# One reference token per block for the scan's scores, with the level-wise scan kept behind a branch, and sample states in fp32

## The chip, the cores and the metric

The kernel runs on one core of one Trainium2 chip. Its time is the device time of one execution in microseconds (us), lower is better. TensorE (PE) multiplies, VectorE (DVE) and ScalarE (ACT) work element by element, GpSimd (POOL) fills constants and issues some transfers, SyncE (SP) issues the others.

## The reference

One decoder layer is applied to 256 prompt tokens and to 32 sample tokens (8 sequences of 4): a SwiGLU feed-forward part, a mixer of two recurrences, and a second feed-forward part. All is fp32. The mixer's heads compute

```python
def gated_linear_scan(q, k, v, log_a, s0):
    """S_t = diag(exp(log_a_t)) S_{t-1} + k_t^T v_t ; o_t = q_t S_t."""
...
        diff = cum[:, :, :, None, :] - cum[:, :, None, :, :]
        decay = jnp.where(causal, jnp.exp(jnp.where(causal, diff, 0.0)), 0.0)
        scores = jnp.sum(qi[:, :, :, None, :] * ki[:, :, None, :, :] * decay, axis=-1)
        o = (jnp.einsum('bhts,bhsv->bhtv', scores, vi)
             + jnp.einsum('bhtd,bhdv->bhtv', qi * jnp.exp(cum), s))
...
        s_new = (jnp.exp(last[:, :, 0, :])[..., None] * s
                 + jnp.einsum('bhsd,bhsv->bhdv', ki * jnp.exp(last - cum), vi))
```

`cum` is the running sum of the log decays. The score of token t on token s therefore holds exp(cum_t - cum_s) for each of 128 key channels. There are 4 GLA heads (key width 128, value width 256, log decay = log-sigmoid / 16) and 8 HGRN heads (128 and 128; the lower bound of the gate is zero at depth one, so the log decay is a plain log-sigmoid). Prompt sequences start from zero states, sample sequences from given ones; final states of both are outputs.

## The kernel before

**Products with weights.** Activations are kept transposed, 128 channels by 288 tokens (256 prompt, 32 sample). Each weight tile is loaded by SP (lines 61 and 63, three buffers `raw`), split into a high and a low part by ACT (`wh`, line 86) and DVE (`wl`, line 87), and used in three PE products per 128x128 tile (lines 464 to 466, in the type that PE takes in one pass). `block` runs these products, four output tiles wide, and calls a `tick` after every 128 input rows, that is after every 12 products.

**The scans.** There are six scans, two heads each: two for GLA, four for HGRN. Each is a Python generator, and a `tick` advances the first one by one `yield`, so a scan's small products stand between the large ones of the blocks `qk1`, `v1`, `hfq`, `hi` and `gate`. The framework's scheduler may still move an instruction within an engine's program. Per scan:

- Scores, level by level: `own` (line 804) for a token with itself, then for h = 1, 2, ... 128 `score` multiplies the keys of the left halves with the queries of the right halves (line 839, four products of 64 columns; line 832 for h = 128; lines 845 and 849 for the samples at h = 1 and 2), `put` copies the valid entries into the score tile `Dg` or `Ds` with a mask (line 864 and others), and `update` (lines 820 to 824) multiplies the decay of one more level into queries, keys and the decay products `F`. No exponent of a positive number is ever taken.
- Output: `out` (lines 933 to 937) multiplies scores with values.
- Sample states: a state tile of 128x512 fp32 is loaded, `halve` (lines 959 and 960) splits it into high and low parts on ACT and DVE, and `sample` multiplies both by the masked queries `qm` (line 978, 64 weight columns, 256 moving columns, four per state tile). Lines 970 and 973 form the new state's update, line 982 adds it on DVE, line 984 stores it from POOL's queue. `inter_a` and `inter_b` (line 996) bring the result back to the transposed layout.
- `final` (line 946) forms the prompt's final state, `norm_a` to `norm_c` the head norm.

**Setup and end.** `setup` fills constants on POOL after the first norm of the mixer. The program's last work is `finish`, whose stores SP issues (lines 650 and 654).

Of the kernel before, what the change touches and what calls it, by code (L numbers as in the profile page):

```python
# [16 lines left out]
P = 128  # L17
# [17 lines left out]
X_EARLY = 12  # L35

# [77 lines left out]

@with_exitstack
def trunk_kernel(ctx, tc, x_prompt, x_sample, state_gla, state_hgrn, norm_gains, f1_in, f1_out, f2_in, f2_out,
                 mix_in, gla_up, gla_b, gla_norm, hgrn_gamma, hgrn_norm, mix_out, masks,
                 y_prompt, y_sample, sgp, shp, sgs, shs):
    nc = tc.nc
    V, S, G, PE = nc.vector, nc.scalar, nc.gpsimd, nc.tensor  # L120

# [535 lines left out]
    def mixer(pn, border):  # L657
        with ExitStack() as mx:
# [5 lines left out]
            def scan_pool():  # L664
                border.pools.close()
                sp.append(mx.enter_context(tc.tile_pool(name="scan", bufs=2, side="right", reuse_waits="tile")))
                its.append(sp[0].tile([P, 256], F32, name="it", bufs=1))
                for i in range(2):
                    vs32.append(sp[0].tile([P, 512], F32, name=f"vs{i}", bufs=1))

                    qm.append(sp[0].tile([P, 9 * 64], F32R, name=f"qm{i}", bufs=1))
            ones = {dv: cst.tile([P, P], F32R, name=f"ones{dv}") for dv in (256, 128)}
            mk = cst.tile([P, 576], U8, name="mk")
# [8 lines left out]
            Dg = cst.tile([P, 2, 2, P], F32, name="Dg")  # L682
            Ds = cst.tile([P, 2, TS], F32, name="Ds")
            Dflat = Dg.rearrange("p i a c -> p (i a) c")

            def setup():
                mi32 = sp[0].tile([P, 576], mybir.dt.int32, name="mi32", tag="Q", bufs=1)
# [3 lines left out]
                G.dma_start(mi32, masks[:, 0:576])  # L691
# [15 lines left out]
                G.tensor_copy(mk, mi32)  # L707
                for a in range(2):
                    G.memset(qm[a].bitcast(F32), 0.0)
                V.tensor_tensor(sel, ident[:, 0:TS], ident[:, TS:2 * TS], op=ALU.add)  # L710
                G.tensor_copy(bmask, bm32)
# [53 lines left out]
            def log_sigmoid(out, z):  # L765

                e = tmp.tile([P, T], F32, name="ls", tag="ls")
                S.activation(e, z, AF.Abs)
                act(e, e, AF.Exp, scale=-1.0)
                act(e, e, AF.Ln, bias=1.0)  # L770
                V.scalar_tensor_tensor(out, z, 0.0, e, op0=ALU.min, op1=ALU.subtract)

            def scan(d, Vt, V32, Vs, gla, ytile0, s0, sp_out, ss_out):
# [246 lines left out]
                def norm_c(a):  # L1020
                    r0 = tmp.tile([P, T], F32, name="r0", tag="lsg")
                    r1 = tmp.tile([P, T], F32, name="r1", tag="ls")
                    act(r0, mss[a][:, 0:T], AF.Ln, bias=epst)
                    act(r0, r0, AF.Exp, scale=-0.5)

                    S.activation(r1, r0, AF.Square)
                    V.scalar_tensor_tensor(r1, mss[a][:, 0:T], EPS, r1, op0=ALU.add, op1=ALU.mult)
                    V.scalar_tensor_tensor(r1, r1, -3.0, r0, op0=ALU.add, op1=ALU.mult)
                    for j in range(nv):
                        yt = y[ytile0 + a * nv + j]  # L1030
                        V.scalar_tensor_tensor(yt, yt, hgain[:, j:j + 1] if gla else hgain[:, 2:3], r1,
                                               op0=ALU.mult, op1=ALU.mult)
# [8 lines left out]
                for a in range(2):  # L1041
                    for b0 in range(0, NB, nb):
                        if b0 + nb < NB:
                            apart(a, b0 + nb)
                            halve(a, b0 + nb)
                        if b0 == 0:
                            final(a)
                        sample(a, b0)
                        if a == 0 and b0 == nb:
                            tp = key_t(1)  # L1050
                        yield
                        if a == 0 and b0 == nb:
                            key_e(1, tp)
                    if a == 0:
                        apart(1, 0)
                        halve(1, 0)
                    inter_a(a)
                    yield
                    inter_b(a)
                    norm_a(a)  # L1060
                    later.append([lambda: None, lambda: None, lambda a=a: norm_b(a), lambda a=a: norm_c(a)])
                    yield
                    if a == 0:
                        out(1)
                        yield
# [47 lines left out]
            def gla_decay(d, g):  # L1113
                for f in range(2):
# [5 lines left out]
                    log_sigmoid(z, z)  # L1120
                    act(d["f"][:, f, :], z, AF.Exp, scale=1.0 / 16.0)

            def ev_hgrn(d, g):
                def ev(f, ps):
# [14 lines left out]
                    V.tensor_scalar(d["f"][:, f, :], ls, omlb[:, hd:hd + 1], lb[:, hd:hd + 1], op0=ALU.mult, op1=ALU.add)  # L1139
                return ev  # L1140

            for g in range(2):
# [14 lines left out]
                gens.append((g, scan(d, *vt, True, 4 * g, state_gla[0][:, 2 * g:2 * g + 2],  # L1157
                                     sgp[0, 0, 2 * g:2 * g + 2], sgs[0][:, 2 * g:2 * g + 2]), True))
            ds, vts = {}, {}
            for kind, g in HORDER:  # L1160
# [8 lines left out]
                for j in list(ds):  # L1169
                    if j // 2 in vts:  # L1170
                        c = slice((j % 2) * 256, (j % 2 + 1) * 256)
                        vt, v32, vs = vts[j // 2]
                        gens.append((2 + j, scan(ds.pop(j), vt[:, :, c], v32[:, c], vs[:, c], False, 8 + 2 * j,
# [34 lines left out]

            for n in range(4):
                block(f"gate{n}", KT, xrhs, ev_gate(n), tick=(tick, tick, tick_silu, tick_last)[n])  # L1210
            for t in range(12, KT):
                split_y(t)
            act_set(AF.Sqrt)
# [70 lines left out]
```

## Time and profile before

| | |
|---|---|
| median of 3 runs | 2307.12 us (2306.62 to 2309.29) |
| span of the profiled execution, first to last instruction | 2303.8 us |
| median less span | 3.3 us |
| granted TensorE clock, mean | 0.998 |
| PE busy | 2287.0 us, 99% |
| DVE busy | 1415.0 us, 61% |
| ACT busy | 1018.9 us, 44% |
| POOL busy | 50.8 us, 2% |
| HBM | 363.62 MB read, 11.80 MB written |

The span is what the profile shows; the run's time has also what lies around it. A PE row's duration is that of one product through the array, and products overlap, so the time that a product holds PE is read from the distance between two starts. One fp32 product of the program makes two records (x8 in the trace for x4 in the program), one with high-low parts makes one, a transpose makes one.

### The profile page before, as it was taken

How to read it: one execution, taken by the hardware profiler on the slowest of the kernel's cores; microseconds unless marked ns; L12 is line 12 of the kernel's file. 1: busy time of each engine (PE TensorE's matmuls, PEld its weight loads, DVE VectorE, ACT ScalarE, POOL GpSimd, SP SyncE). 2: the span in 40 equal slices, each digit the busy share in tenths (PEclk: the TensorE clock that was granted, in tenths of full speed). 3: DMA queues.
4: the chain of work that ended last, by engine and by line, in shares of the span. 5: the costliest groups of instructions: out<-in, count | busy, mean ns of one | idle time of the engine just before them, and what ended most of it. 6: DMA issues, size and time to landing. Idle time of an engine off the chain costs nothing.

```text
span 2303.8 us, 42125 instructions
## 1 busy us (share of the span) xinstructions
PE 2287.0 (99%) x17352; PEld 2274.0 (99%) x17352; DVE 1415.0 (61%) x2303; ACT 1018.9 (44%) x1567; POOL 50.8 (2%) x97
## 2 busy tenths in 40 slices
PE   9999999999999999999999999999999999999998
PEld 8999999999999999999999999999999999999998
DVE  7545545554556468788888754854555455545545
ACT  6443333333334445454556654544333333333345
POOL 0000000000000001000000000100000000000000
PEclk9999999999999999999999999999999999999999
DMA  7555555555555545456465555455555555555553
GB/s 216 165 165 165 165 166 166 167 166 168 166 165 184 165 152 164 142 163 181 144 173 155 161 185 160 136 164 168 165 165 166 167 163 164 165 165 165 165 165 115
DMA packets 217008, 378.16 MB, mean 164 GB/s; under 512 B 15362, under 2 KB 52400, under 8 KB 216816
## 3 DMA queue, kind: packets, MB, share of 16 engines
q1 hardware_dynamic: 211264, 365.48, 52.4%
q0 software_dynamic: 3376, 9.81, 1.3%
q8 instruction: 136, 2.23, 0.4%
q10 hardware_dynamic: 2176, 0.18, 0.1%
q14 instruction: 56, 0.46, 0.1%
HBM read 363.62 MB, written 11.80 MB: 163 GB/s over the span
## 4 chain that ended last, share of the span: by engine, by line
PE 88%; issue 7%; DVE 2%; DMA 1%; POOL 1%; ACT 1%; DVEq 0%; POOLq 0%; ACTq 0%; SPq 0%
PE gate L464 9%; PE gate L466 9%; PE gate L465 9%; PE out L465 8%; PE out L466 8%; PE out L464 8%; PE up L466 8%; PE up L464 8%; PE up L465 8%; PE mo L466 1%; PE mo L464 1%; PE mo L465 1%; PE hfq L464 1%; PE hfq L465 1%; PE hfq L466 1%
## 5 line engine op out<-in xcount | busy, mean ns | idle before, releaser
L87 DVE TENSOR_TENSOR wl<-raw,wh 128x1024 fp32r<-128x1024 f32 (+1 forms) x674 | 821.7, 1220 | 627.4 <-ACT wh L86 624.7
L86 ACT ACTIVATE wh<-raw 128x1024 fp32r<-128x1024 f32 (+1 forms) x674 | 711.3, 1056 | 1067.3 <-PE gate L465 318.4
L465 PE MATMUL gate<-xl,wh 128*128 128x288 f32 x1660 | 489.1, 295 | 0.1
L466 PE MATMUL gate<-xh,wl 128*128 128x288 f32 x1660 | 489.1, 295 | 0.0
L464 PE MATMUL gate<-xh,wh 128*128 128x288 f32 x1660 | 488.6, 296 | 0.0
L465 PE MATMUL out<-hl,wh 128*128 128x288 f32 x1408 | 415.8, 295 | 0.0
L464 PE MATMUL out<-hh,wh 128*128 128x288 f32 x1408 | 415.6, 295 | 0.0
L466 PE MATMUL up<-xh,wl 128*128 128x288 f32 x1408 | 415.0, 295 | 0.0
L466 PE MATMUL out<-hh,wl 128*128 128x288 f32 x1408 | 415.0, 295 | 0.0
L464 PE MATMUL up<-xh,wh 128*128 128x288 f32 x1408 | 414.6, 294 | 0.3 <-DVE g L523 0.3
L465 PE MATMUL up<-xl,wh 128*128 128x288 f32 x1408 | 414.8, 295 | 0.0
L465 PEld LDWEIGHTS gate<-xl,wh 128*128 128x128 f32 x1660 | 311.9, 188 | 1.0 <-DVE xl L243 0.9
L466 PEld LDWEIGHTS gate<-xh,wl 128*128 128x128 f32 x1660 | 311.7, 188 | 0.0
L464 PEld LDWEIGHTS gate<-xh,wh 128*128 128x128 f32 x1660 | 310.6, 188 | 0.7 <-ACT xh L242 0.2
L464 PEld LDWEIGHTS out<-hh,wh 128*128 128x128 f32 x1408 | 264.6, 188 | 0.2 <-DVE u L531 0.2
L466 PEld LDWEIGHTS out<-hh,wl 128*128 128x128 f32 x1408 | 264.7, 188 | 0.0
L464 PEld LDWEIGHTS up<-xh,wh 128*128 128x128 f32 x1408 | 264.1, 188 | 0.6 <-DVE g L523 0.5
L465 PEld LDWEIGHTS out<-hl,wh 128*128 128x128 f32 x1408 | 264.5, 188 | 0.0
L466 PEld LDWEIGHTS up<-xh,wl 128*128 128x128 f32 x1408 | 264.2, 188 | 0.1
L465 PEld LDWEIGHTS up<-xl,wh 128*128 128x128 f32 x1408 | 264.1, 188 | 0.1
L583 DVE TENSOR_TENSOR y<-out,y 128x288 f32<-128x288 f32 x288 | 121.5, 452 | 104.5 <-PE out L466 101.7
L464 PE MATMUL hfq<-xh,wh 128*128 128x288 f32 x256 | 78.4, 306 | 0.0
(341 smaller groups left out, 2560.1 us busy)
## 6 DMA issues: line engine op xcount, KB each, us to landing
raw<-in_ffn_w_in_dram SPq DMA_DIRECT2D x352, 512.0 KB, 3.6
raw<-in_ffn_w_out_dram SPq DMA_DIRECT2D x176, 512.0 KB, 3.7
raw<-in_mix_w_in_dram SPq DMA_DIRECT2D x64, 512.0 KB, 3.7
raw<-in_mix_w_in_dram SPq DMA_DIRECT2D x96, 256.0 KB, 3.3
raw<-in_mix_w_out_dram SPq DMA_DIRECT2D x32, 512.0 KB, 3.7
out_dram<-s POOLq DMA_DIRECT2D x32, 256.0 KB, 3.1
s<-in_state_gla_dram SPq DMA_DIRECT2D x16, 256.0 KB, 4.0
s<-in_state_hgrn_dram SPq DMA_DIRECT2D x16, 256.0 KB, 3.3
```

Source lines behind the costliest of these rows:

```text
L86: i1 = self.nc.scalar.activation(h[:, c], raw[:, c], AF.Copy).ins
L87: i2 = self.nc.vector.tensor_tensor(l[:, c], raw[:, c], h[:, c].bitcast(F32), op=ALU.subtract).ins
L464: yield lambda: PE.matmul(dst, w[0][:, c:c + P], parts[0], start=start, stop=False)
L465: yield lambda: PE.matmul(dst, w[0][:, c:c + P], parts[1], start=False, stop=False)
L466: yield lambda: PE.matmul(dst, w[1][:, c:c + P], parts[0], start=False, stop=stop)
L583: V.tensor_tensor(y[k], ps, y[k], op=ALU.add)
```

## The change

`trunk_kernel` becomes a wrapper. It allocates `span` and `over`, runs the whole layer once (`trunk`, with `block_scan`), loads `over` into a register of every engine and, under `tc.If`, runs the whole layer again with the old scans. The second copy is in the program as a block that is jumped over when `over` is 0.

`block_scan` takes the place of `scan` in the first run. A running sum of the log decay is made by two instructions on DVE (`tensor_tensor_scan`), reset at each block of tokens: 256 for GLA, 64 for HGRN, 4 for a sample sequence. The sum at the block's middle token is subtracted, the queries are multiplied by exp(sum), the keys by exp(-sum), and the scores of a block are one product and one masked copy. For HGRN, factors between neighbouring blocks of 64 (`g6`, `g7`, `gk`, `gs`) give the other scores. The largest distance from the middle token is collected in `span` and compared with 60 at the end of the mixer; beyond that `over` is 1. Sums are clamped to ±60. The gates hand over the log decay rather than the decay.

The sample states stay in fp32: `run` multiplies all eight states of a head, one after the other, with 32 weight columns each, into four different groups of 32 output partitions in turn, and four products add the samples' own scores. State buffers `s0` go from 5 to 8, and loads are issued in the scan's first steps. `mi32` and its mask load go; `block_masks` makes the masks on POOL.

```diff
+def trunk_kernel(tc, *args):
+    with tc.tile_pool(name="guard", bufs=1) as pool:
+        span = pool.tile([P, 2, 12], F32, name="span")
+        over = pool.tile([1, 1], mybir.dt.int32, name="over")
+        trunk(tc, *args, (span, over))
+        again = tc.nc.values_load(over[0:1, 0:1], min_val=0, max_val=1)
+        with tc.If(again > 0, preferred_fallthrough_block=False):
+            trunk(tc, *args, None)
...
+            def block_scan(d, Vt, V32, Vs, gla, ytile0, s0, sp_out, ss_out):
...
+                for a in range(2):
+                    V.tensor_tensor_scan(f[:, a, :], resets[0 if gla else 1], f[:, a, :], 0.0, op0=ALU.mult, op1=ALU.add)
+                load_state()
+                yield
+                for x_, c in zip(blocks(f), (0, n)):
+                    h = x_.shape[3] // 2
+                    V.tensor_copy(col(mid, c, x_.shape[2]), x_[:, :, :, h - 1:h])
+                    V.tensor_tensor(x_, x_, col(mid, c, x_.shape[2]).broadcast_to(x_.shape), op=ALU.subtract)
+                for x_, c in zip(blocks(f), (0, 4)):
+                    s_ = col(span, c, x_.shape[2])
+                    for i, u in ((0, unit), (x_.shape[3] - 1, -unit)):
+                        V.scalar_tensor_tensor(s_, x_[:, :, :, i:i + 1], u, s_, op0=ALU.mult, op1=ALU.max)
+                V.tensor_scalar(f, f, SPAN / unit, -SPAN / unit, op0=ALU.min, op1=ALU.max)
+                act(ep, f, AF.Exp, scale=unit)
+                act(A, mid, AF.Exp, scale=unit)
...
+                act(f, f, AF.Exp, scale=-unit)
...
+                V.tensor_tensor(k, k, f, op=ALU.mult)
...
+                if gla:
+                    for a in range(2):
+                        ps = auxtile("sc")
+                        PE.matmul(ps[:, 0:TP], k[:, a, 0:P], q[:, a, 0:TP], start=True, stop=True, skip_group_check=True)
+                        PE.matmul(ps[:, TP:3 * P], k[:, a, P:TP], q[:, a, P:TP], start=False, stop=True,
+                                  skip_group_check=True)
+                        own(ps, a)
+                        V.copy_predicated(Dg[:, a], tri, ps[:, 0:3 * P])
+                        own_put(ps, a, a + 1)
+                        yield
+                else:
+                    for i in range(2):
+                        ps = auxtile("sc")
+                        for a in range(2):
+                            PE.matmul(ps[:, a * 192:(a + 1) * 192], k[:, a, i * P:(i + 1) * P], Qv[:, a, i, :],
+                                      start=a == 0, stop=True, skip_group_check=True)
...
+                    ps = auxtile("sc7")
+                    for a in range(2):
+                        PE.matmul(ps[:, a * P:(a + 1) * P], Kd[:, a, 0:P], q7[:, a, :], start=a == 0, stop=True,
+                                  skip_group_check=True)
...
+                def run(a):
+                    ss = auxtile("os")
+                    w = dv // 4
+                    for b in range(NB):
+                        r = slice(b % 4 * TS, (b % 4 + 1) * TS)
+                        PE.matmul(ss[r, 0:dv], qm[0][:, a, b * TS:(b + 1) * TS], states[a, b // nb * nb][:, b % nb, :],
+                                  start=b < 4, stop=False, skip_group_check=True)
+                    for i in range(4):
+                        PE.matmul(ss[i * TS:(i + 1) * TS, i * w:(i + 1) * w], Ds[:, a, :],
+                                  V32[:, a * dv + i * w:a * dv + (i + 1) * w], start=False, stop=True, skip_group_check=True)
+                    it = sp[0].tile([P, dv], F32, name="it", tag="it", bufs=1)
+                    S.activation(it, ss[:, 0:dv], AF.Copy)
+                    its_[a] = it
+
+                def out(a):
+                    po = auxtile("o")
+                    for j in range(nv):
+                        v = [Vt[:, t, a * dv + j * P:a * dv + (j + 1) * P] for t in range(2)]
+                        PE.matmul(po[:, j * TP:(j + 1) * TP], v[0], Dg[:, a, 0:TP], start=j == 0, stop=False,
+                                  skip_group_check=True)
+                        PE.matmul(po[:, j * TP + P:(j + 1) * TP], v[1], Dg[:, a, TP:3 * P], start=False, stop=True,
+                                  skip_group_check=True)
```

Three places show how the instructions move. The first is PE's program at the first HGRN scan's scores, before (`Q` and `k_h` are the queries and keys with the decay so far, 127x64 is the size of the result; the rows of the blocks between are left out):

```order
L804 MATMUL sc_d<-q_h_10939,k_h_10940 128x128 x4
...
L839 MATMUL sc_11921<-Q,k_h_10940 127x64 x4
L845 MATMUL sc_11921<-Q,k_h_10940 32x16 x2
L849 MATMUL sc_11921<-q_h_10939,k_h_10940 32x32 x2
...
L839 MATMUL sc_11964<-Q,k_h_10940 126x64 x4
L845 MATMUL sc_11964<-Q,k_h_10940 32x16 x2
...
L839 MATMUL sc_11999<-Q,k_h_10940 124x64 x4
```

The same place on PE now (`Qv` holds the queries with the factor to the block's middle, `Kd` the keys carried to the half's end):

```order
L1249 MATMUL sc<-Qv,k_h_10833 128x192 x2
L1228 MATMUL sc<-rp,k_h_10833 32x32 x2
...
L1249 MATMUL sc<-Qv,k_h_10833 128x192 x2
...
L1264 MATMUL sc_11854<-q_h_10832,Kd 128x128 x2
```

Nine stops of PE between the blocks' products become three, and 40 products become 8.

The second place is PE at the sample states of the first HGRN scan, before (`hl` is a split state, `qm` the masked queries, `sn` the new state's update):

```order
L973 MATMUL sn<-bd,ks 128x512
L978 MATMUL os<-hl,qm_9574 64x256 x4
L464 MATMUL hfq_0_11877<-xh_137,wh_12066 128x288
...
L973 MATMUL sn<-bd,ks 128x512
L978 MATMUL os<-hl,qm_9574 64x256 x4
```

And now, for the second head of that scan (`s` is a state as loaded, `Ds` the samples' own scores):

```order
L1347 MATMUL sn<-bd,ks 128x512
L1301 MATMUL os<-s_11952,qm 32x128 x4
L1301 MATMUL os<-s_12004,qm 32x128 x4
L1304 MATMUL os<-vs_9581,Ds 32x32 x4
L479 MATMUL hi_0_12123<-xh_130,wh_11899 128x288
```

The state products no longer stand with each state's update; eight of them and four more follow each other without a large product between.

The third place is DVE at the start of the first HGRN scan, now (`small` holds the block factors, `s` states and `sn` updates of the GLA scan before it):

```order
L1187 TENSOR_TENSOR Qv<-q_h_10832,ep 128x4x128
L1188 TENSOR_TENSOR rp<-q_h_10832,ep 128x64
L1193 TENSOR_TENSOR k_h_10833<-k_h_10833,f_h_10834 128x576
...
L1213 TENSOR_TENSOR Kd<-k_h_10833,small 128x512
L1215 TENSOR_TENSOR q_h_10832<-Qv,small 128x2x128
...
L1350 SCALAR_TENSOR_TENSOR s_11212<-s_11212,small,sn 128x256 x2
L1291 TENSOR_TENSOR bd<-ks,bmask 96x256
```

The scan's whole preparation stands on DVE ahead of the last four state updates of the GLA scan before it, while PE's score products of this scan stand behind that scan's last products.

On SP one register load of `over` stands between two loads of `mix_w_out` weights; on the other engines it stands at the end of the program, ahead of the branch.

More of the change, by code (lines that the diff above doesn't have):

```diff
@@ L35 @@
 X_EARLY = 12
+SPAN = 60.0
 class Weights:
@@ L706, in setup @@
                 G.memset(Ds, 0.0)
-                G.tensor_copy(mk, mi32)
-                for a in range(2):
-                    G.memset(qm[a].bitcast(F32), 0.0)
+                if not blockwise:
+                    G.tensor_copy(mk, mi32)
+                for t in qm:
+                    G.memset(t.bitcast(F32) if t.dtype == F32R else t, 0.0)
                 V.tensor_tensor(sel, ident[:, 0:TS], ident[:, TS:2 * TS], op=ALU.add)
+                if blockwise:
+                    for i in (2, 3):
+                        V.tensor_tensor(sel, sel, ident[:, i * TS:(i + 1) * TS], op=ALU.add)
                 G.tensor_copy(bmask, bm32)
@@ L1020, in norm_c @@
                 def norm_c(a):
[L1021 to L1032, printed above, removed]
+                    head_norm(mss[a], [y[ytile0 + a * nv + j] for j in range(nv)], gla)
                 tp = key_t(0)
```

284 lines of the change are left out of this document (269 added, 15 removed).

## The prediction

> **What bounds the kernel now.** The page of the profile comes first: its head, its first part (busy time by engine) and its fourth (the chain of work that ended last, by engine).
>
> ```profile
> span 2303.8 us, 42125 instructions
> PE 2287.0 (99%) x17352; PEld 2274.0 (99%) x17352; DVE 1415.0 (61%) x2303; ACT 1018.9 (44%) x1567; POOL 50.8 (2%) x97
> PE 88%; issue 7%; DVE 2%; DMA 1%; POOL 1%; ACT 1%; DVEq 0%; POOLq 0%; ACTq 0%; SPq 0%
> ```
>
> PE is busy all the time and carries the chain. The change lies in the mixer, so the second view is the windows: the mixer as a whole, a stretch full of scans, and one behind the last scan. The columns are the length, then busy time and instruction count of PE, PEld, DVE, ACT and POOL.
>
> ```profile
> 860.00:1440.00 580.00, 578.17 (x4477) 568.96 (x4476) 450.80 (x949) 311.61 (x635) 37.41 (x62) 1.00 0.54 162
> 1240.00:1300.00 60.00, 60.00 (x474) 58.83 (x474) 51.39 (x120) 34.44 (x75) 4.11 (x6) 1.00 0.48 140
> 1300.00:1360.00 60.00, 60.00 (x454) 60.00 (x454) 40.16 (x62) 36.70 (x56) 0.00 (x0) 1.00 0.59 185
> ```
>
> In the mixer PE misses 1.8 of 580 us, at a granted clock of 1.00. DVE comes next with 51.39 of 60 us where scans run and 40.16 where none does. A product taken from PE there is time taken from the kernel, as long as nothing else becomes later than PE; work taken from DVE, ACT or a DMA is not.
>
> **How I price a product.** The timeline of PE gives start and duration; what counts is the distance between starts. In steady state products of 288 columns stand 0.13 us apart. This is a stretch with `own` of one scan and the large products behind it:
>
> ```profile
> 1239.14 1.05 PE L804 MATMUL sc_d<-q_h,k_h 128*128 128x128 f32 x8
> 1239.95 0.38 PE L464 MATMUL gate<-xh,wh 128*128 128x288 f32 x1
> 1240.17 0.29 PE L465 MATMUL gate<-xl,wh 128*128 128x288 f32 x1
> 1240.29 0.29 PE L466 MATMUL gate<-xh,wl 128*128 128x288 f32 x1
> ```
>
> Four fp32 products (eight records) start at 1239.14, the next large one at 1239.95, and that one holds PE 0.22 us and not 0.13. So the stop costs 0.81 + 0.09 = 0.90 us, 0.225 a product of 128 columns. I use the same sum, distance plus 0.09, for each stop.
>
> **Scores.** Level h = 1, h = 4, h = 64 and h = 128 of a scan, each with the row that follows it:
>
> ```profile
> 1241.62 0.99 PE L839 MATMUL sc<-Q,k_h 128*127 128x64 f32 x8
> 1242.54 0.30 PE L845 MATMUL sc<-Q,k_h 128*32 128x16 f32 x4
> 1242.69 0.29 PE L849 MATMUL sc<-q_h,k_h 128*32 128x32 f32 x4
> 1242.91 0.40 PE L464 MATMUL gate<-xh,wh 128*128 128x288 f32 x1
> 1251.99 0.98 PE L839 MATMUL sc<-Q,k_h 128*124 128x64 f32 x8
> 1252.78 0.38 PE L466 MATMUL gate<-xh,wl 128*128 128x288 f32 x1
> 1266.31 0.68 PE L839 MATMUL sc<-Q,k_h 128*64 128x64 f32 x8
> 1266.92 0.40 PE L465 MATMUL gate<-xl,wh 128*128 128x288 f32 x1
> 1267.95 0.67 PE L832 MATMUL sc<-Q,k_h 128*128 128x128 f32 x4
> 1268.37 0.38 PE L466 MATMUL gate<-xh,wl 128*128 128x288 f32 x1
> ```
>
> That makes 1.38 for h = 1, 0.88 for h = 4, 0.70 for h = 64, 0.51 for h = 128. For h = 2 I take 1.2 (h = 1 without line 849), for the three levels between h = 4 and h = 64 their mean, 0.79 each. With `own`: 0.90 + 1.38 + 1.2 + 0.88 + 2.37 + 0.70 + 0.51 = 7.9 us a scan, 47.6 us for six.
>
> What replaces them needs a price for 256 columns. The prompt's final state of a GLA scan has it (two products, four records):
>
> ```profile
> 954.47 1.11 PE L946 MATMUL st<-Vg,kd 128*128 128x256 f32 x4
> 955.24 0.57 PE L970 MATMUL sn<-Vsg,bd 96*128 96x256 f32 x2
> ```
>
> 0.77 + 0.09 is 0.43 a product; 192 columns lie midway to 0.225, at 0.33. The samples' own scores have 32 weight columns: line 849 takes 0.22 + 0.09 = 0.31 for two, and the four products before line 845 take 0.92 where those at h = 4 take 0.79, so entering the 32-column form costs about 0.1. A GLA head then costs 0.43 + 0.225 + 0.26 = 0.92, an HGRN scan 4 x 0.33 + 0.41 + 2 x 0.225 = 2.2. Four heads and four scans: 12.3 us. The scores give back 47.6 - 12.3 = 35.3 us.
>
> **Outputs.** Lines 933 to 937 and the state products after them:
>
> ```profile
> 1211.80 0.38 PE L933 MATMUL o<-Dg,Vh 128*128 128x128 f32 x2
> 1212.24 0.39 PE L935 MATMUL o<-Dg,Vh 128*128 128x128 f32 x2
> 1212.46 0.31 PE L937 MATMUL os<-Ds,vs 128*128 128x32 f32 x2
> 1212.60 0.66 PE L978 MATMUL os<-hl,qm 128*64 128x256 f32 x4
> 1213.10 0.29 PE L464 MATMUL gate<-xh,wh 128*128 128x288 f32 x1
> ```
>
> 0.80 us for a head and half of 128 values, 16 of them. Now it is one product of 256 and one of 128 columns, 0.655: 2.3 us back. (Line 937's part is counted in `run`.)
>
> **Sample states.** From the same rows, the four products of line 978 take 0.50 us; at a GLA scan, in the first two rows here, 0.48. The third row groups all of them:
>
> ```profile
> 970.26 0.64 PE L978 MATMUL os<-hl,qm 128*64 128x256 f32 x4
> 970.74 0.29 PE L464 MATMUL v<-xh,wh 128*128 128x288 f32 x1
> L978 PE MATMUL os<-hl,qm 128*64 128x256 f32 x128 | 20.7, 282 | 0.0
> ```
>
> 32 stops of four, 15.4 us, go. `run` brings, for each of four GLA heads, eight fp32 products of 256 columns and four of 64; for each of eight HGRN heads eight of 128 and four of 32. If each waits for the one before it, that is 8 x 0.43 + 4 x 0.11 = 3.9 us a GLA head and 8 x 0.215 + 4 x 0.07 = 2.0 an HGRN head (0.11 between the 32-column price and that of 128 columns), 32 us in all, and 12 stops with two changes of form and a late large product, 0.3 each, 3.6 us. So 36 us in turn, and fp32 states are then 20 us worse than split ones.
>
> But consecutive products of `run` use four different strips of 32 output columns, and nothing in this trace does. Line 978 uses the first 64 columns alone, lines 845 and 849 the first 32, one after the other. The bounds are thus one product at a time (36 us) and four at a time (8 + 3.6 = 11.7 us). Between them I use the records: each fp32 product is two passes, both on the same strip and in program order, so the second pass of one can lie beside the first pass of the next, but not beside its own first. That hides half: 16 + 3.6 = 19.8 us. I take it as an estimate.
>
> The Trainium skill, "TensorEngine Tiling (Array Packing)", section Key Properties, says that tiles work independently and load and multiply in parallel, and that a change of tiling mode drains the engine. On the first, `run` would cost 11.7 us rather than 19.8; no run here shows it so far. On the second the trace agrees (the 0.1 us into the 32-column form).
>
> PE's sum: 35.3 + 2.3 + 15.4 - 19.8 = 33.2 us less.
>
> **What is hidden, and what is not.** The split of states (lines 959 and 960, 24.0 and 25.2 us on ACT and DVE), masked copies and level updates go; running sums, exponentials and factors come. They lie beside PE in both kernels. DVE loses, per scan, nine steps of two multiplications and a masked copy, and gains some nine wide operations:
>
> ```profile
> L959 ACT ACTIVATE hl<-s 128x256 fp32r<-128x256 f32 x64 | 24.0, 408 | 15.2 <-PE os L978 10.6 <-DMA s<-in_state_hgrn_dram 3.4 <-DMA s<-in_state_gla_dram 0.9
> L960 DVE TENSOR_TENSOR hl<-s,hl 128x256 fp32r<-128x256 f32 x64 | 25.2, 417 | 0.2
> L820 DVE TENSOR_TENSOR Q<-Q,F 128x256 f32<-128x256 f32 (+1 forms) x36 | 15.4, 427 | 15.5 <-PE sc L839 13.0 <-PE sc L845 2.4
> L882 DVE TENSOR_TENSOR Q<-q_h,f_h 128x576 f32<-128x576 f32 x4 | 3.0, 752 | 0.0
> L149 ACT ACTIVATE ls<-ls 128x288 f32<-128x288 f32 x56 | 22.5, 433 | 0.4
> ```
>
> No row shows a running sum; the nearest, 128x288 elementwise, takes 0.45 us, and up to double that changes nothing while PE bounds. What can cost is the chain from the running sum to the first score product: sums, subtraction, clamp, exponential on ACT twice, two multiplications, the block factors. At 0.45 to 0.9 for each sum, 0.75 for each wide step and 0.9 for each wide exponential (two of 0.433), with a dozen small ones of 0.2, it is about 9 us long. The generator gives it five or six steps of 12 products, 8 to 9.5 us; but in the program DVE does it ahead of the last four state updates of the scan before. I book 2 us for waits on it, between -2 (the waits that PE had in the mixer, 1.8 us) and 10.
>
> SP now waits for `over` with weight loads behind it. The longest wait of SP for a split is in this row, and PE does not wait behind it:
>
> ```profile
> SPq L63 <- DVE wl L87: 1258.7, 443, 13.7
> ```
>
> `over` stands some nine DVE instructions behind the split that frees the next buffer, about 6 us; three raw and four split tiles of 3.2 us lie ahead of PE. I book nothing, and 6 us as the bound without that cover.
>
> At the end every engine branches over the second copy of the layer, SP last. Its last rows:
>
> ```profile
> 2297.73 1.41 DVE L642 SCALAR_TENSOR_TENSOR zT<-zT,rc,xT 128x512 f32<-128x512 f32 x2
> 2299.68 0.89 SPq L654 DMA_DIRECT2D out_dram<-zT  x2
> ```
>
> SP issues until 2300.57 and the span ends at 2303.8, while the stores land. The other engines' register load and branch fit into that; SP's far jump comes after the landing. No row has such a jump: its bounds are nothing and the 3.2 us that a transfer and the end take here; I take 2. The Trainium skill, "Runtime: NRT & Kernel Launch", section Instruction fetch mechanics, says that a taken branch out of the prefetched window forces a fetch of the target before execution goes on; that would lie within these bounds, and no run here shows it yet.
>
> **The sum.** 33.2 - 2 - 2 = 29.2 us less: a span of 2274.6 in place of 2303.8, and with the 3.3 us that lie around it 2277.9, say 2278 us.
>
> **The rivals.**
> - *All four strips at once.* `run` costs 11.7, PE saves 41.3, the kernel 37.3: 2270 us. For it: different strips share neither weight columns nor output partitions. Against: two passes per product in program order. The Trainium skill, "TensorEngine Tiling (Array Packing)", section Key Properties, states it as a rule.
> - *The strips in turn.* `run` costs 36, PE saves 17, the kernel 13: 2294 us. For it: no rows of this trace lie side by side, and half the weight columns (line 978) gave no discount, 0.12 us a record of 256 columns against 0.13 of 288.
> - *The scan's start becomes a wait (slower).* If DVE, 86% busy where scans run, stretches the 9 us chain to twice its length and the scheduler's lead does not help, PE waits some 9 us at each of six starts, 54 us: 2278 + 54 = 2332. It decides against the change from (29 + 4.6) / 6 = 5.6 us a scan on. Against it: the preparation stands far ahead on DVE, and the kernel before had a DVE step between any two levels and lost 1.8 us.
> - *The guard fires and the layer runs twice,* some 4600 us. The log decay is a log-sigmoid of a value of about unit spread, near -0.8 a token; 32 tokens from the middle of an HGRN block make 26, 128 of GLA 6.5 after the sixteenth, both well below 60.
>
> **How the numbers follow.** The chances: half hidden 0.45, four at once 0.25, in turn 0.22, a wait that takes most of the gain 0.03, slower 0.04 (the guard in it below 0.01), the rest near no change. The range reaches from 2262 (four at once, no booked waits, and the scores' stops 4 us cheaper than priced) to 2298 (in turn, with 4 us more of wait or tail) and leaves out under 2 in 10. A difference of about 0.2%, 4.6 us, is what a measurement of this kernel can tell from none; the three cases that hold 0.92 are all faster than that. Faster 0.93, same 0.03, slower 0.04.
>
> **What would show it.** PE stays at 99% and the mixer's window shrinks by some 31 us, while both feed-forward stages keep their length. The distance from the first row of `run` to the large product after it decides the main question: about 3.9 us for a GLA head says in turn, 2.1 half, 1.1 four at once. Stops for scores: two of 0.9 us per GLA scan, three of 0.5 to 1.1 per HGRN scan. Idle PE ahead of line 1238, 1249 or 1301 with DVE or ACT as releaser would show the wait; a longer stretch behind the last store, the jump. The prediction is wrong in its reasons if PE's count falls as said and the time does not.

## The result, and the profile after

| | before | after |
|---|---|---|
| median | 2307.57 us (4 runs, 2306.62 to 2309.29) | 2273.29 us (4 runs, 2271.34 to 2274.15) |
| span of the profiled execution | 2303.8 us | 2272.4 us |
| first product of `qk` to the first product of the second feed-forward part (the mixer) | 584.1 us | 545.2 us |
| from there to PE's last product | 855.1 us | 855.1 us |
| from PE's last product to the end (the tail) | 9.4 us | 16.3 us |

The ratio is 0.985 (95% interval 0.9836 to 0.9864): faster by 34 us, where 29 were forecast. The profiled run of before had 3.3 us around its span, the 27 later runs of before and every other kernel about 1.7 to 1.9; so spans are what is to be compared. The forecast span was 2274.6, the measured one 2272.4. Two errors cancel in that: the mixer became nearly 8 us shorter than forecast, the tail 5 us longer. That the total came out so near is luck.

First the page of the changed kernel, its head, busy times and chain:

```profile
span 2272.4 us, 41304 instructions
PE 2245.2 (99%) x17057; PEld 2230.2 (98%) x17057; DVE 1364.7 (60%) x2164; ACT 1007.0 (44%) x1513; POOL 54.0 (2%) x109
PE 94%; DVE 2%; DMA 1%; ACT 1%; issue 1%; DVEq 0%; SPq 0%; ACTq 0%
```

PE is as full as before and the chain lies on it even more. Next the windows: the mixer, and 3.3 us inside it (columns as in the prediction; the three numbers at the end are granted clock, DMA share and GB/s).

```profile
860.00:1401.70 541.70, 536.51 (x4186) 524.75 (x4185) 401.34 (x812) 300.06 (x582) 39.20 (x64) 1.00 0.59 173
1110.30:1113.60 3.30, 3.30 (x17) 3.26 (x17) 2.28 (x7) 0.54 (x2) 0.00 (x0) 0.53 0.00 0
```

PE now misses 5.2 us in the mixer where it missed 1.8, and for 3.3 us its clock is near half. The run of a GLA head stands in the timeline like this (line 1301 are the state products, 1304 the samples' own scores, 479 to 481 the large products):

```profile
945.39 0.29 PE L481 MATMUL qk<-xh,wl 128*128 128x288 f32 x1
945.61 1.07 PE L1301 MATMUL os<-s,qm 128*32 128x256 f32 x16
946.50 0.29 PE L1304 MATMUL os<-vs,Ds 128*32 128x64 f32 x8
946.72 0.40 PE L479 MATMUL qk<-xh,wh 128*128 128x288 f32 x1
946.96 0.29 PE L480 MATMUL qk<-xl,wh 128*128 128x288 f32 x1
```

From 945.61 to the next large product it is 1.11 us: the number that the prediction gave for four strips at once. Its sixteen records of 256 columns take 0.89 us, in groups of four whose starts are 7 ns apart, one group every 0.216 us. These are the groups for `run`, the scores of HGRN and the running sum, and PE's waits on them:

```profile
L1301 PE MATMUL os<-s,qm 128*32 128x128 f32 (+1 forms) x192 | 9.4, 314 | 0.0
L1304 PE MATMUL os<-vs,Ds 128*32 128x32 f32 (+1 forms) x96 | 3.1, 203 | 0.0
L1249 PE MATMUL sc<-Qv,k_h 128*128 128x192 f32 x32 | 7.5, 362 | 3.2 <-DVE Qv L1204 3.2
L1164 DVE TENSOR_TENSOR_SCAN f_h<-reset,f_h 128x288 f32<-128x288 f32 x8 | 5.9, 749 | 0.3 <-ACT f_h L164 0.3
```

```profile
PE sc L1249 <- DVE Qv L1204: 3.2, 2, 2.6
```

**Where PE's time went.** The same sum as in the prediction (distance between starts, plus what the large product behind a stop holds above 0.13 us), over all rows of the mixer:

| term | forecast | measured |
|---|---|---|
| scores | 47.6 to 12.3: 35.3 back | 48.0 to 13.0: 35.0 back (at full clock) |
| outputs and the samples' own scores | 2.3 back | 14.3 to 10.4: 3.9 back |
| state products | 15.4 to 19.8: 4.4 lost | 15.4 to 10.6: 4.8 back |
| state updates, final states, all other rows | not in the sum | 1.1 back, 1.1 lost, 0.8 lost |
| PE in the mixer | 33.2 back | 42.9 back |
| waits, and the half clock behind one | 2 lost | about 4 lost |
| tail | 2 lost | 6.9 lost |

Measured scores after are taken from the run with the loads on POOL, below, in which the clock did not fall; in the changed kernel itself they are 14.3.

**The stop.** At the second HGRN scan PE waits 2.6 us for `Qv`. (At the first, whose score products start at 1062.2, it does not wait. Expectations below that speak of "the first HGRN scores" mean this place.) Going back from there, the timelines of SP, ACT, DVE and PE of the changed kernel (1140 is a state load, 62 a weight load, 87 and 88 a weight split; 164 the exponential, 1187 its use):

```profile
1100.05 0.37 SPq L1140 DMA_DIRECT2D s<-in_state_hgrn_dram  x1
1100.52 1.98 SPq L62 DMA_DIRECT2D raw<-in_mix_w_in_dram  x4
```

```profile
1105.33 1.06 ACT L87 ACTIVATE wh<-raw 128x1024 fp32r<-128x1024 f32 x1 [4.61 <-DMA raw<-in_mix_w_in_dram]
1106.30 0.67 ACT L164 ACTIVATE ep<-f_h 128x576 f32<-128x576 f32 x1
```

```profile
1107.00 0.69 DVE L1187 TENSOR_TENSOR Qv<-q_h,ep 128x512 f32<-128x512 f32 x1 [2.89 <-ACT ep L164]
```

```profile
1109.42 0.92 PE L1249 MATMUL sc<-Qv,k_h 128*128 128x192 f32 x4 [2.62 <-DVE Qv L1204]
1110.27 0.31 PE L1228 MATMUL sc<-rp,k_h 128*32 128x32 f32 x4
1110.51 1.65 PE L1249 MATMUL sc<-Qv,k_h 128*128 128x192 f32 x4
1111.95 1.06 PE L1264 MATMUL sc<-q_h,Kd 128*128 128x128 f32 x4
```

SP issues the state load at 1100.05, and the weight load that ACT waits for stands behind it. ACT waits 4.61 us for that weight and only then makes the exponential, which stands behind the split in its program; DVE waits 2.89 us for the exponential, PE for DVE. The last two rows show what comes on top: the same product as at 1109.42 now takes 1.65 us instead of 0.92, because the clock has fallen at 1110.47. What SP waited for is in its waits:

```profile
SPq L1140 <- DMA out_dram<-s: 40.9, 17, 6.1
```

Seventeen of the state loads wait for the store of the state that held their buffer, 40.9 us in all; the longest wait, 6.1 us, is that of the load issued at 1100.05. Such waits are not new. The kernel before has more of them, and there PE misses only 1.8 us in the whole mixer:

```profile
SPq L796 <- DMA out_dram<-s: 71.5, 23, 7.8
```

What is new is the chain behind them, from the weight by way of ACT's exponential to PE's next products. The rest of the 5.2 us that PE misses is mostly 0.6 us for another `Qv` and 1.2 us for `k_g` at the mixer's start; some of the later runs do not have the second.

**The tail.** SP's last stores and, from the view by source line (count, duration, first and last start), its instructions at the branch (line 124) and in the program's last block (line 1635):

```profile
2255.39 6.00 SPq L669 DMA_DIRECT2D out_dram<-zT  x6
2261.48 2.40 SPq L665 DMA_DIRECT2D out_dram<-zS  x4
2264.30 1.32 SPq L669 DMA_DIRECT2D out_dram<-zT  x2
```

```profile
L124 SPq EVENT_SEMAPHORE  x8: 17/17/17, 2265.8 to 2268.0; - x8
L124 SPq COMPARE_BRANCH  x2: 41/47/53, 2265.7 to 2268.0; - x2
```

```profile
L1635 SPq EVENT_SEMAPHORE  x14: 17/28/28, 2270.8 to 2272.4; - x14
```

The same stores in the kernel before (the last row of them stands in the prediction):

```profile
2293.65 3.86 SPq L654 DMA_DIRECT2D out_dram<-zT  x6
2297.85 1.74 SPq L650 DMA_DIRECT2D out_dram<-zS  x4
```

The stores take 9.7 us to issue where the same twelve took 6.5; one of them alone takes 2.60 us. Each engine has two branch instructions. On SP the second stands behind the waits for the stores, and between it and the first instruction of the last block lie 2.7 us: the jump over the second layer. SP's stores were slow while the other engines were already jumping: ACT leaves the branch at 2257.2, DVE at 2261.0.

### The profile page after: what moved, and what is told of

Its sections match the earlier page's. It is cut to its first block, busy times and chain, and to the rows that moved or that the text cites. A ratio compares the mean times of both kernels' runs of the same rounds, so it can differ in the third digit from the quotient of the medians.

```text
span 2272.4 us, 41304 instructions
## 1 busy us (share of the span) xinstructions
PE 2245.2 (99%) x17057; PEld 2230.2 (98%) x17057; DVE 1364.7 (60%) x2164; ACT 1007.0 (44%) x1513; POOL 54.0 (2%) x109
## 4 chain that ended last, share of the span: by engine, by line
PE 94%; DVE 2%; DMA 1%; ACT 1%; issue 1%; DVEq 0%; SPq 0%; ACTq 0%
PE gate L479 9%; PE gate L481 9%; PE gate L480 9%; PE out L480 8%; PE out L481 8%; PE out L479 8%; PE up L481 8%; PE up L479 8%; PE up L480 8%; PE mo L481 1%; PE mo L479 1%; PE mo L480 1%; PE hfq L479 1%; PE hfq L480 1%; PE hfq L481 1%; ACT wh L87 1%
```

## The experiments

Every kernel below was timed beside the kernel before on the same chip. Mixer and tail are those of the first table, in the profiled execution, in us. "Stop" is the distance between PE's two starts ahead of the second HGRN scan's first scores where it is over 1 us; "half clock" is how long the clock stood at 0.50 around its end.

| kernel | median us | ratio (95%) | mixer | tail | stop | half clock |
|---|---|---|---|---|---|---|
| after | 2273.29 | 0.985 (0.9836 to 0.9864) | 545.2 | 16.3 | 2.9 | 3.4 |
| after, once more | 2272.08 | 0.9847 (0.9834 to 0.9859) | 544.3 | 15.7 | 2.1 | 3.4 |
| one strip | 2295.06 | 0.9948 (0.9932 to 0.9965) | 566.4 | 16.8 | none | none |
| pairs | 2270.95 | 0.9848 (0.9831 to 0.9864) | 541.5 | 14.2 | 1.4 | none |
| states only | 2299.08 | 0.9966 (0.9954 to 0.9979) | 577.9 | 9.7 | none | none |
| no branch | 2266.65 | 0.9825 (0.9808 to 0.9841) | 547.6 | 9.6 | 3.1 | 6.8 |
| short block | 2267.07 | 0.9823 (0.9806 to 0.9839) | 545.0 | 10.7 | 2.4 | 3.4 |
| early jump | 2267.54 | 0.983 (0.9813 to 0.9846) | 541.5 | 13.2 | 2.7 | none |
| loads on POOL | 2269.33 | 0.9838 (0.9822 to 0.9855) | 540.7 | 14.5 | none | none |
| both | 2267.64 | 0.9831 (0.9819 to 0.9844) | 540.5 | 13.6 | none | none |

Runs of one kernel lie 2 to 5 us apart, so medians 1 us apart are not told apart; what a change does is read from mixer and tail, each of one profiled run.

**One strip.** All products of `run` go to the same 32 output partitions; the number of products and of columns stays.

```diff
-                        r = slice(b % 4 * TS, (b % 4 + 1) * TS)
+                        r = slice(0, TS)
...
-                                  start=b < 4, stop=False, skip_group_check=True)
+                                  start=b == 0, stop=False, skip_group_check=True)
...
-                        PE.matmul(ss[i * TS:(i + 1) * TS, i * w:(i + 1) * w], Ds[:, a, :],
+                        PE.matmul(ss[0:TS, i * w:(i + 1) * w], Ds[:, a, :],
```

> All products of run go to the first strip of 32 output partitions; number, sizes and order stay. Theory A (products on four different strips lie beside each other): without different strips each waits for the one before it, run of a GLA head goes from 1.1 us to about 4.0 and of an HGRN head from 0.7 to about 2.1, 4 x 2.9 + 8 x 1.4 = 23 us more, time about 2296. Theory B (a product with 32 weight columns is short wherever it goes): run stays at 1.1 us and the time within 2 us of 2273. My forecast's pairs (second pass of one beside the first of the next) need different strips too, so this run does not tell them from A.

The same place in its timeline, and its groups:

```profile
944.43 3.64 PE L1301 MATMUL os<-s,qm 128*32 128x256 f32 x16
947.91 0.61 PE L1304 MATMUL os<-vs,Ds 128*32 128x64 f32 x8
948.45 0.40 PE L479 MATMUL qk<-xh,wh 128*128 128x288 f32 x1
```

```profile
L1301 PE MATMUL os<-s,qm 128*32 128x128 f32 (+1 forms) x192 | 30.0, 310 | 0.0
L1304 PE MATMUL os<-vs,Ds 128*32 128x32 f32 (+1 forms) x96 | 5.8, 203 | 0.0
```

4.02 us a GLA head instead of 1.11, and 35.8 us of rows instead of 12.5, each row as long as before (310 ns against 314): nothing in a product changed but what it stands beside. Priced as in the prediction, from start to start, `run` takes 34.1 us instead of 10.6. The mixer is 21.2 us longer and the kernel 21.8, although this run has neither the stop nor the half clock. That settles the main question: four strips work at once.

**Pairs.** The eight states go to strips 0, 0, 1, 1, 2, 2, 3, 3 instead of 0, 1, 2, 3, 0, 1, 2, 3.

```diff
-                    for b in range(NB):
+                    for b in (0, 4, 1, 5, 2, 6, 3, 7):
```

> The eight states of a head go to the strips in the order 0,0,1,1,2,2,3,3 in place of 0,1,2,3,0,1,2,3. If PE takes products in program order and only neighbours can lie beside each other, two in a row on one strip wait: about half of the gain of four strips goes, run of a GLA head 1.1 to about 2, 4 x 1 + 8 x 0.5 = 8 us more, about 2281. If PE looks further ahead than one product, run stays near 1.1 us and the time within 2 us of 2273.

The state products of all heads span 7.2 us from start to start in both kernels, so two neighbours on the same strip cost nothing: PE does not need the strips in turn. The time is no worse than that of the changed kernel. In what order the two passes of a product go the trace does not say.

**States only.** The kernel before, level by level, with nothing of the change but the fp32 states and `run` (its state buffers go to eight as well, no guard, no second copy).

```diff
-                            PE.matmul(pos[a][1][0:2 * TS, 0:TP], w, hl[n // 2][:, n % 2 * TP:(n % 2 + 1) * TP],
-                                      start=False, stop=b0 + i == NB - 1, skip_group_check=True)
...
+                        PE.matmul(ss[r, 0:dv], qm[0][:, a, b * TS:(b + 1) * TS], states[a, b // nb * nb][:, b % nb, :],
+                                  start=b < 4, stop=False, skip_group_check=True)
```

> The level-wise scores of the kernel before, with the fp32 states of the change: eight products per head on four strips, no split of states, eight state buffers; no guard and no branch. Theory A (strips at once): line 978's 15.4 us and line 937's 2.2 go, run's 9.5 come: 8 us less than before, about 2299. If the states were the change's loss and the scores its whole gain (strips in turn): 18 us more than before, about 2326. The distance from here to e3_no_branch is then what the scores give, about 31 us by A.

7.4 us less than before: fp32 states pay by themselves. (In turn, at the 34.1 us of the run in one strip, their products would have cost 19 us more than the 15.4 of the split ones.) Its rows for `run` are those of the changed kernel, 9.4 and 3.1 us. The run without the branch differs from it by the scores, the products of the output and the guard's sums; together these bring 32.4 us, stops and half clock included.

**No branch.** The guard's values are computed, but not loaded, and the second copy is left out.

```diff
-        again = tc.nc.values_load(over[0:1, 0:1], min_val=0, max_val=1)
-        with tc.If(again > 0, preferred_fallthrough_block=False):
-            trunk(tc, *args, None)
```

> The register loads, the branch and the second copy of the layer are left out; the guard's span is still collected and compared. Theory A (the end lost what the mixer gained: fetches of the jump's target, 2.7 us on SP itself and the rest by late stores): the stretch from the last PE product to the end goes from 16.3 back to 9.4 us, span 2265.5, time about 2268. Rival (only SP's own jump counts): 2.7 us less, 2270.6. Rival (the end costs nothing and the late stores were chance): 2273.

6.6 us less than the changed kernel, 5.4 less than its repetition. The tail is that of before (9.6 against 9.4), and so are the stores:

```profile
2257.49 3.86 SPq L666 DMA_DIRECT2D out_dram<-zT  x6
2261.68 1.75 SPq L662 DMA_DIRECT2D out_dram<-zS  x4
2263.54 0.87 SPq L666 DMA_DIRECT2D out_dram<-zT  x2
```

**Short block.** The block under the branch is one small store in place of the second layer (the second run is left out). What is computed, loaded and compared stays.

```diff
-            trunk(tc, *args, None)
+            tc.nc.sync.dma_start(args[17][0, 0:P, D - 24:D], span.rearrange("p a c -> p (a c)"))
```

> The branch and the register loads stay, but the guarded block is one small store, so the jump over it is a few instructions long; the second run of the layer is left out. Theory A (what the end costs is the fetch of a far target, on all engines): the end is as long as without a branch, 9.4 to 10.5 us from the last product, about 2268. Rival (register load and branch themselves cost it): 16 us, 2273.

The same register loads and the same branch, taken over a short distance, leave a tail of 10.7 us. Branching thus costs 1.1 us of it, and the length of what is jumped over 5.6. The 1.1 us look like the stores again: the twelve take 7.6 us to issue, and one of them 1.56.

**Early jump.** The whole second layer stays, but it follows the branch directly, and the ordinary way jumps over it at once; SP's waits for the last stores, and the program's last block, lie behind the jump.

```diff
-        with tc.If(again > 0, preferred_fallthrough_block=False):
+        with tc.If(again > 0, preferred_fallthrough_block=True):
```

> The second copy of the layer is the block that follows the branch, and the block taken here lies behind it, next to the end. There is still one far jump on each engine, but SP's comes before it waits for the last stores and not after. Theory A (2.7 us of SP's jump lie open behind the stores): about 2.5 us less, 2270.8, and the late stores stay. Rival (the jump waits for the stores' traffic wherever it is): 2273.

The view by source line again, and the stores:

```profile
L124 SPq EVENT_SEMAPHORE  x8: 17/17/17, 2262.7 to 2263.3; - x8
L124 SPq COMPARE_BRANCH  x1: 50/50/50, 2259.8 to 2259.8; - x1
```

```profile
L1635 SPq EVENT_SEMAPHORE  x14: 17/28/28, 2263.3 to 2264.9; - x14
```

```profile
2251.07 4.47 SPq L669 DMA_DIRECT2D out_dram<-zT  x6
2255.63 1.96 SPq L665 DMA_DIRECT2D out_dram<-zS  x4
2258.01 1.76 SPq L669 DMA_DIRECT2D out_dram<-zT  x2
```

There is one branch now, and the jump is still there: SP branches at 2259.8, and its next instruction starts at 2262.7, 2.9 us later. (On ACT and DVE it is 4.1 and 4.0 us.) But SP jumps while its stores are still landing, the last at 2261.9, so that only 0.8 us of it lie open, and no second jump follows. The stores take 8.2 us, between 6.5 and 9.7. The tail is 3.1 us shorter; but kernels that end like the changed one (one strip, pairs, loads on POOL) have tails from 14.2 to 16.8 us, and only 1 us of the 3.1 lies beyond that spread. The time is 5.7 us shorter, more than I expected, because the mixer is 3.7 us shorter too: the stop of 2.7 us stood there but the clock did not fall behind it, and a wait of 1.2 us at the mixer's start is missing. Neither has to do with the order of blocks at the program's end as far as the trace shows; the last section says why the clock stayed up.

The pages of these kernels hold one more trace of the cause, the instruction fetches of one queue (packets, MB, share): before, after, without the branch, with the short block, with the early jump.

```profile
q14 instruction: 56, 0.46, 0.1%
```

```profile
q14 instruction: 64, 0.52, 0.1%
```

```profile
q14 instruction: 55, 0.45, 0.1%
```

```profile
q14 instruction: 56, 0.45, 0.1%
```

```profile
q14 instruction: 63, 0.52, 0.1%
```

Seven or eight packets more, of 8 KB each, where a long block is jumped over. They fall into the tail. So do blocks of 16 KB on the other queue of instructions, q8: three in the changed kernel, two with the early jump, one with the short block, none without the branch or in the kernel before, where no store is slow. Over all eleven traces, from 10 us on, 89 of SP's issues take more than 0.7 us, and 82 of them overlap a block of q8; of all its issues 11% do. So slow issues and fetches go together, in the mixer too; that the one slows the other is not shown by a run of its own.

**Loads on POOL.** The state loads of the first run are issued by POOL, so that weight loads no longer stand behind them.

```diff
-                        nc.sync.dma_start(t, s0[b0:b0 + nb, a].rearrange("b p v -> p b v"))
+                        G.dma_start(t, s0[b0:b0 + nb, a].rearrange("b p v -> p b v"))
```

> The sample states are loaded from POOL's queue and not from SP's; nothing else. Theory A (a state load that waits on SP for its buffer's store holds back the weight loads behind it, these hold ACT's split, and the scan's exponential stands behind that): SP's 40.9 us of waits for stores of states and PE's waits of 3.2 us for line 1204 go, the mixer gets about 3 us shorter, time about 2270. Rival (the exponential chain itself is too long): PE's waits stay, time 2273. If states now come too late for run, PE waits there and the time rises.

The chain of the stop, in this kernel:

```profile
1102.53 1.06 ACT L87 ACTIVATE wh<-raw 128x1024 fp32r<-128x1024 f32 x1 [2.01 <-PE hi L480]
1103.49 0.67 ACT L164 ACTIVATE ep<-f_h 128x576 f32<-128x576 f32 x1
```

```profile
1106.62 0.92 PE L1249 MATMUL sc<-Qv,k_h 128*128 128x192 f32 x4
1107.47 0.31 PE L1228 MATMUL sc<-rp,k_h 128*32 128x32 f32 x4
1107.71 0.92 PE L1249 MATMUL sc<-Qv,k_h 128*128 128x192 f32 x4
1108.46 0.61 PE L1264 MATMUL sc<-q_h,Kd 128*128 128x128 f32 x4
```

ACT no longer waits for the weight but for PE, the exponential is 2.8 us earlier, PE does not stop, and its second product takes 0.92 and not 1.65 us. The mixer is 4.5 us shorter: 2.8 of it the stop, 1.7 the half clock.

**Both, and the changed kernel once more.** The last two repairs together, and the changed kernel between the same runs.

> Both of the last two repairs: the state loads of the first run are issued by POOL instead of SP, and the blocks are ordered so that the end of the program follows the branch without a jump. Theory A (SP standing at a state load makes the weights late, PE then stops 2.9 us and its clock falls to 0.50 for 3.4 us behind the stop; the tail is a separate matter): the mixer is 42.6 us shorter than before as with the loads on POOL alone, in every run, and the tail 13.2 us as with the blocks reordered alone: a span of about 2265, a time near 2266.7, with a spread below 2 us. Rival (the two gains, 4.0 and 5.7 us, are independent and add up): 2263.6. Rival (both gains were only the variation from run to run of the changed kernel): 2271 to 2273.

> The changed kernel once more, on the same chip and between the same runs as the two repairs together, since the differences in question (2 to 6 us) are as large as its own spread. Theory A: 2271 to 2274, with the stop of 2 to 3 us ahead of the first HGRN scores and a granted clock of 0.50 behind it in the profiled execution. Rival (the clock fell by chance in the first profile): no stretch of half clock in the mixer, and a time near 2270.

The changed kernel gave 2272.08 with a stop of 2.1 us and 3.4 us of half clock; so these belong to it and were no accident of the first profile. Both repairs together have a span of 2264.9 in the profiled execution, as expected, and a time of 2267.64, 4.4 us below the changed kernel and no better than the early jump alone. The spread of its times is 2.3 us, a little over the 2 that I expected. The gains do not add up, because the mixer of the kernel with the early jump had lost its half clock already (541.5 against 540.5 us). These two are the best times of a kernel that keeps the guard and the second layer, some 39 us below the kernel before.

## Why the forecast came out, and what in it was wrong

- **PE bounds the kernel; only what is taken from PE counts.** Right. PE stayed at 99%, the feed-forward part ahead of the mixer kept its length to 0.3 us, the one behind it to 0.1.
- **Scores.** Right to 0.3 us, since both sides were a little higher than priced, by 0.4 and 0.7 us. Pricing a stop as distance plus the longer hold of the next product carried over to shapes the trace did not have.
- **Outputs.** 3.9 instead of 2.3: the stops of one typical place, times sixteen, missed 1.5 us elsewhere, some 0.9 of it products for the samples' own scores.
- **Sample states.** This is the step that failed: "That hides half: 16 + 3.6 = 19.8 us. I take it as an estimate." It measured 10.6. The estimate supposed that a product's second pass must wait for its own first and that order in the program binds the passes; the rows show four records at a time from the first group to the last, and the pairs show that the order does not matter. What happened is the rival of four strips at once, which had 11.7 and a chance of 0.25; its forecast for the whole, 2270 us, was missed the other way, by the tail. The price in turn, 36, is near what the run in one strip shows (34.1). By the sentence of the Trainium skill that tiles work independently ("TensorEngine Tiling (Array Packing)", Key Properties), `run` would have cost 11.7 and the trace agrees with 10.6. Its other rule, the drain at a change of mode, agrees with the large product ahead of `run`, which holds PE 0.22 us (945.39 to 945.61) and not the 0.13 that it holds ahead of products of 128 columns. Behind `run` a large product holds 0.24 us, but behind fp32 products of 128 columns it is 0.22 as well.
- **The wait at a scan's start.** The size was near (2 booked, about 4 measured with the half clock), the cause was not. I feared a chain of DVE steps that is too long; DVE was early enough. The wait came through SP: a state load that waits for its buffer holds up the weight loads behind it, and the exponential stands behind a weight's split on ACT. I weighed `over` on SP as such a wait (it cost nothing) and not the state loads that the change moved to the scan's first steps. The state loads as such were no danger before; what makes them one is the exponential in the chain to PE. The chain itself takes 17 us from running sum to `Qv` rather than 9 in this scan (15 with the loads on POOL, 9 to 21 in the others), since the steps of other work lie between its own; a running sum takes 0.75 us, within its bounds.
- **The tail.** Both ends of my bounds, nothing and 3.2 us, held for the jump alone (2.7), but not for the stores, which had been no part of the step: 3.2 us more to issue. The rule of the Trainium skill on a taken branch out of the prefetched window ("Runtime: NRT & Kernel Launch", Instruction fetch mechanics) agrees: from SP's branch to its next instruction it is 2.7 us over the long block, 0.2 over the short one.
- **The guard** did not fire; the time would have been twice as long.

So the sum of PE was 9 to 10 us too careful, waits and tail 7 us too kind. The lower end of the range is 2 us too low by its own terms: 2270, less 2 of waits and 4 of scores, is 2264, not 2262.

## What to carry to other kernels

Products that go to different strips of 32 output columns are to be priced as groups of four, one group for the price of one product, in both orders tried here. A transfer that has to wait for its buffer does not belong on the queue that feeds the bounding engine, once a chain to that engine stands behind what the queue brings, and a stop of TensorE can cost more than its length. A jump over a long block that is hardly ever run cost SP, ACT and DVE 2.7 to 4.1 us here wherever it stood; it belongs where other work, such as the landing of the last stores, still covers it.

## What the runs showed of the hardware

- Stops of 2.1, 2.4, 2.9 and 3.1 us were followed by 3.4, 3.4, 3.4 and 6.8 us at half clock, one of 2.7 us by none. In three of the four the clock fell about 1 us after PE had begun again (in the changed kernel at 1110.47, PE having started at 1109.42), in the longest 0.6 us before. The Trainium skill, "TensorE: Matmul & The Clock Gate", Part 1, has the clock halved after an idle window of about 3.4 us that runs freely, whatever the kernel does. One and two such windows are the lengths at half clock here. But no stop was as long as a window, and in three of the four PE had worked in the last microsecond of it: here the measurement differs, and a shorter stop is enough if it falls badly.
- What "badly" means can be read off the traces. The time between two changes of the clock is always a whole number of steps of 3.413 us (1099.09 us, for one, is 322 of them), so they lie on a grid. In the steps just ahead of the four falls in the mixer PE's rows cover 31, 36, 38 and 48% of the time. In no other step of any mixer, in eleven traces, do they cover less than 51% at full clock. The stop of 2.7 us was cut by the grid: 56% of one step and 73% of the next were covered. In the longest half clock the step after the fall was covered to 82% only, and the clock came back one step later. So where a stop lies on the grid decides, and that is chance. The cover is no exact measure: at the program's end, among rows of a single column and transposes, the clock also falls behind steps that are covered to 94%.
- Four products in different strips start 7 ns apart, the next four 0.216 us later.
- One store's issue on SP took 2.60 us in the tail, where others take 0.33 to 0.43. It overlaps a 16 KB fetch of instructions, like 82 of the 89 slow issues in all traces.
